# The moving weight operand of a hybrid decoder layer read in turns from two halves of a block

## The chip, the cores and the metric

The kernel runs on one NeuronCore of a Trainium2 chip. The metric is the device time of one execution in microseconds. Three executions of the kernel before took 367.40, 367.41 and 368.95 us; the median is 367.41 us.

## What is computed

One decoder layer on 256 rows of width 1024: an input projection, two attention mixers side by side, a gated merge, a feed-forward part, and a last norm. Cut to what matters here:

```python
h = rmsnorm(x, norm1_g)                       # x: 256 x 1024
proj = h @ w_in                               # 1024 x 4888: q, k/v, gates, q/k/v, merge gates
y_nsa, y_moba = nsa_attention(...), moba_attention(...)
mixed = sig(g_nsa) * (y_nsa @ w_up_nsa) + sig(g_moba) * (y_moba @ w_up_moba)
x = x + mixed @ w_out
u = relu(rmsnorm(x, norm2_g) @ w_ff1)         # 1024 x 4096
x = x + (u * u) @ w_ff2                       # 4096 x 1024
out = rmsnorm(x, norm_f_g)
```

All inputs are float32. Some 66 MB of weights pass through the core once.

## The kernel before

**Three products for one.** Every float32 operand of a large matrix product is split into a high part and a low part of type fp32r: ScalarE (ACT) copies the loaded block `raw` into `whi` (the copy rounds), VectorE (DVE) writes `wlo = raw - whi`. `mm3` (line 245) then issues three matmuls into one accumulator: high times high, high times low, low times high. Each goes through `mm` (line 242).

**Stationary and moving.** TensorE loads a 128x128 block first (LDWEIGHTS, engine PEld in the profile) and then streams the columns of the other operand past it (MATMUL, engine PE). A row `acc<-whi,hTh 128*128 128x512` reads: into `acc`, moving operand `whi` with 512 columns, stationary operand `hTh`. There are two kinds of stage, and only the first concerns the change:

- *The weights move.* `xstat` (line 256) multiplies the normed input, stationary in `hTh`/`hTl`, by the weight chunks `kva`, `kvb`, `q`, `qm`, `km`, `vm` (two chunks each). A chunk holds four blocks of `n` neighbouring columns, `n` = 384, 408 or 512, for four slices of the contraction; both halves of the 256 rows use each block. `seven_mms` (line 998) and `ff2_mms` (line 1039) multiply the squared activations, stationary in `ah`/`al`, by the chunks of `w_ff2`. `seven_mms` serves chunks 0 to 13: it forms seven products in place of eight, from blocks of 512 columns, three read from the chunk itself (`sh`, `sl`) and four from sums of its blocks (`wt`, split again into `whi`, `wlo`). `ff2_mms` serves the last two chunks without that. `mm3_halves` (line 250) is `mm3` with the 512 columns as two matmuls of 256; it stands at the end of a stage, so that half of a bank is complete earlier.
- *The weights stand still.* `wstat` (line 272) is used for the merge gates, the two up projections, `w_out` and `w_ff1`. There the activations move, 256 columns at a time.

**What sets the order.** The order is written by hand. Each chunk has a slot: `run_slot` (line 228) issues the slot's matmuls, and between them, at positions given as shares of the slot, the evacuations, splits and loads that `at` put into it. The engines run on their own behind semaphores. Loads go through SP's queue into three `raw` buffers, five chunks ahead; `whi` and `wlo` have three buffers each. From about 205 us on the slots alternate: one `w_ff1` chunk (48 matmuls, activations moving), then one `w_ff2` chunk (21 products of 512 columns, weights moving).

**The host's part.** `_layout` (line 1190) arranges the weights in HBM; `_blocks` cuts a matrix into chunks in which every partition's data lies in one run. The elementwise work on a chunk (splits, sums of blocks) treats all columns alike.

## Time and profile before

| view | value |
|---|---|
| device time, median of three | 367.41 us |
| span of the profiled execution, first to last instruction | 366.6 us |
| instructions | 6535 |
| DMA, mean over the span | 181 GB/s, 66.34 MB |
| stage 4.67 to 14.54 us, chunks kva (384 columns move) | 9.87 us, DMA share 1.02 |
| stage 14.54 to 29.80 us, kvb (408 columns move) and other work | 15.26 us, PE busy all of it |
| stage 82.92 to 211.04 us, weights mostly stationary | 128.12 us, PE busy 127.87 us |
| stage 344.49 to 360.00 us, the last two w_ff2 chunks and the end of the product | 15.51 us |

The profiled execution's own time lies 0.8 us above its span when it is taken as the median. [...]

### The profile page before, as it was taken

The numbers are of one execution on the slowest core, as the hardware profiler recorded it, in microseconds if no ns is written. First come the engines' busy times: TensorE is split into PE (matmuls) and PEld (weight loads), VectorE is DVE, ScalarE is ACT, GpSimd is POOL, SyncE is SP. The second block draws the span as 40 slices with busy tenths as digits, with TensorE's granted clock in tenths as the row PEclk, the third lists the DMA queues.
The fourth block names the chain that finished last, engine by engine and source line by source line (L and its number), as shares of the span: only waits on it lengthen the run. The fifth ranks groups of instructions, "written<-read, shape, count | busy, mean of one in ns | idle before, by whom it ended". The sixth has DMA issues, their size and how long they took to land.

```text
span 366.6 us, 6535 instructions
## 1 busy us (share of the span) xinstructions
PE 358.8 (98%) x2663; PEld 330.3 (90%) x2663; DVE 320.1 (87%) x466; ACT 241.4 (66%) x367; POOL 3.4 (1%) x14
## 2 busy tenths in 40 slices
PE   8999999999999999999999999999999999999993
PEld 7997877879999999999999999999999999999983
DVE  4988979998967759767978999999999999999985
ACT  5994765777746657625365988876766677766623
POOL 1010000000000000000000000000000000000000
PEclk9999999999999999999999999999999999999997
DMA  8978426333434333533483556544455665544003
GB/s 283 400 307 312 129 106 228 115 116 115 161 133 168 116 116 126 219 116 114 181 335 137 214 229 221 183 180 179 186 208 224 229 232 229 203 181 181 11 3 114
DMA packets 11262, 66.34 MB, mean 181 GB/s; under 512 B 1248, under 2 KB 2784, under 8 KB 3936
## 3 DMA queue, kind: packets, MB, share of 16 engines
q1 hardware_dynamic: 10368, 64.35, 47.3%
q10 hardware_dynamic: 864, 1.57, 1.2%
q8 instruction: 21, 0.34, 0.4%
q14 instruction: 9, 0.07, 0.1%
HBM read 64.87 MB, written 1.05 MB: 180 GB/s over the span
## 4 chain that ended last, share of the span: by engine, by line
PE 94%; issue 2%; ACT 1%; DVE 1%; POOL 0%; POOLq 0%; DVEq 0%
PE acc L243 61%; PE o L243 10%; PE yb L243 6%; PE tp L243 4%; PE qacc L243 3%; PE kvbacc L243 3%; PE Sa L243 2%; PE Sa L597 1%; PE tp L339 1%; ACT P L567 1%; PE yb L156 1%; PE Sb L597 1%; PE Sb L243 1%; PE o L886 0%; DVE P L581 0%
## 5 line engine op out<-in xcount | busy, mean ns | idle before, releaser
L116 DVE TENSOR_TENSOR wlo<-raw,whi 128x1024 fp32r<-128x1024 f32 (+3 forms) x83 | 104.9, 1285 | 3.3 <-ACT whi L114 3.2
L114 ACT ACTIVATE whi<-raw 128x1024 fp32r<-128x1024 f32 (+3 forms) x82 | 90.0, 1119 | 26.0 <-PE acc L243 11.9
L243 PE MATMUL acc<-h2h,whi 128*128 128x256 f32 x256 | 70.9, 277 | 0.0
L243 PE MATMUL acc<-h2l,whi 128*128 128x256 f32 x256 | 70.7, 276 | 0.0
L243 PE MATMUL acc<-h2h,wlo 128*128 128x256 f32 x256 | 70.7, 276 | 0.0
L243 PEld LDWEIGHTS acc<-h2h,whi 128*128 128x128 f32 x256 | 48.1, 188 | 0.0
L243 PEld LDWEIGHTS acc<-h2l,whi 128*128 128x128 f32 x256 | 48.1, 188 | 0.0
L243 PEld LDWEIGHTS acc<-h2h,wlo 128*128 128x128 f32 x256 | 48.1, 188 | 0.0
L989 ACT ACTIVATE whi<-wt 128x2048 fp32r<-128x2048 f32 x14 | 26.9, 1921 | 28.4 <-PE acc L243 27.3
L243 PE MATMUL acc<-hTh,wlo 128*128 128x256 f32 x128 | 36.6, 286 | 0.0
L243 PE MATMUL acc<-hTh,whi 128*128 128x256 f32 x128 | 35.5, 278 | 0.0
L243 PE MATMUL acc<-hTl,whi 128*128 128x256 f32 x128 | 35.5, 277 | 0.0
L991 DVE TENSOR_TENSOR wlo<-wt,whi 128x2048 fp32r<-128x2048 f32 x14 | 32.0, 2283 | 0.1
L243 PE MATMUL acc<-whi,hTh 128*128 128x512 f32 (+2 forms) x65 | 25.6, 394 | 0.1
L243 PE MATMUL acc<-wlo,hTh 128*128 128x512 f32 (+2 forms) x65 | 25.1, 386 | 0.0
L243 PE MATMUL acc<-whi,hTl 128*128 128x512 f32 (+2 forms) x65 | 24.8, 382 | 0.0
L982 DVE TENSOR_TENSOR sl<-raw,sh 128x1536 fp32r<-128x1536 f32 x14 | 24.5, 1749 | 0.0
L243 PEld LDWEIGHTS acc<-hTh,wlo 128*128 128x128 f32 x128 | 24.1, 188 | 0.2 <-issue 0.2
L243 PEld LDWEIGHTS acc<-hTh,whi 128*128 128x128 f32 x128 | 24.2, 189 | 0.1
L243 PEld LDWEIGHTS acc<-hTl,whi 128*128 128x128 f32 x128 | 24.0, 188 | 0.0
L980 ACT ACTIVATE sh<-raw 128x1536 fp32r<-128x1536 f32 x14 | 20.8, 1489 | 3.2 <-PE acc L243 3.2
L243 PE MATMUL acc<-mxh,whi 128*128 128x256 f32 x64 | 17.7, 276 | 0.0
(310 smaller groups left out, 868.6 us busy)
## 6 DMA issues: line engine op xcount, KB each, us to landing
raw<-in_ff_dram SPq DMA_DIRECT2D x32, 1024.0 KB, 5.1
raw<-in_gm_dram SPq DMA_DIRECT2D x8, 1024.0 KB, 4.8
raw<-in_wout_dram SPq DMA_DIRECT2D x4, 1024.0 KB, 4.8
raw<-in_q_dram SPq DMA_DIRECT2D x2, 1024.0 KB, 5.4
raw<-in_qm_dram SPq DMA_DIRECT2D x2, 1024.0 KB, 6.4
raw<-in_km_dram SPq DMA_DIRECT2D x2, 1024.0 KB, 6.0
raw<-in_vm_dram SPq DMA_DIRECT2D x2, 1024.0 KB, 4.8
raw<-in_upn_dram SPq DMA_DIRECT2D x2, 1024.0 KB, 4.8
```

The lines of the kernel that those rows point to most:

```text
L114: act.activation(hi[c][:, a:b], raw[c][:, a:b], AF.Copy)
L116: dve.tensor_tensor(lo[c][:, a:b], raw[c][:, a:b], hi[c][:, a:b].bitcast(F32), op=ALU.subtract)
L156: pe.transpose(warm[:, 0:128], ident, ident)
L243: pe.matmul(o, l, r, start=start, stop=stop, skip_group_check=True)
L339: pe.transpose(tp[:, j * 256 + t * 128:j * 256 + t * 128 + 128], src[:, t, (2 * i + j) * 128:(2 * i + j + 1) * 128], ident)
L567: act.activation(P[:, 2 * x + j, a:b], S[:, j, x], AF.Exp, scale=0.125, bias=st[:, 1, i:i + 1], accum_out=st[:, 2, i:i + 1])
L597: pe.transpose(T[:, j, x, o:o + 128], P[:, 2 * x + j, c:c + 128], ident)
L980: act.activation(singles[c][0], v, AF.Copy)
L982: dve.tensor_tensor(singles[c][1], v, singles[c][0].bitcast(F32), op=ALU.subtract)
L989: act.activation(hi[c], v, AF.Copy)
L991: dve.tensor_tensor(lo[c], v, hi[c].bitcast(F32), op=ALU.subtract)
```

## The change

In HBM, every block of `n` columns of the chunks `kva`, `kvb`, `q`, `qm`, `km`, `vm` and `ff2` is rearranged: its even columns first, its odd columns behind them. In SBUF a block thus holds column 0, 2, 4, ... in its first half and 1, 3, 5, ... in its second. The matmuls in which these weights move read the two halves in turns, so that the columns come in their old order: first half, second half, first half and so on, two neighbouring reads lying `n/2` elements apart (1024 bytes at `n` = 512, 768 at 384, 816 at 408). The outputs in PSUM stand as before. The number of instructions, their order on every engine, the sizes of all transfers and all tiles are the same. The matmuls of 256 columns read 128 columns from each half of the block.

```diff
+    def paired(v):
+        return v.rearrange("p (a b) -> p b a", a=2)
+
     def mm(o, l, r, start, stop):
+        if len(r.shape) > len(o.shape):
+            o = o.rearrange("p (b a) -> p b a", a=2)
         pe.matmul(o, l, r, start=start, stop=stop, skip_group_check=True)
...
     def mm3_halves(o, lh, ll, rh, rl, first, last):
         r = mm3(o, lh, ll, rh, rl, first, last)[:int(first)]
-        return r + [m for x in (slice(0, 256), slice(256, 512))
-                    for m in mm3(o[:, x], lh, ll, rh[:, x], rl[:, x], first, last)[int(first):]]
+        return r + [m for x in range(2)
+                    for m in mm3(o[:, 256 * x:256 * x + 256], lh, ll,
+                                 *(v[:, 128 * x:128 * x + 128] for v in (rh, rl)),
+                                 first, last)[int(first):]]
...
-                r += f(accs[t][:, :n], lh, ll, h[:, k * n:(k + 1) * n],
-                       l[:, k * n:(k + 1) * n], kt == 0, kt == 7)
+                r += f(accs[t][:, :n], lh, ll, paired(h[:, k * n:(k + 1) * n]),
+                       paired(l[:, k * n:(k + 1) * n]), kt == 0, kt == 7)
...
             if kb < 3:
-                h, l = (x[:, kb * 512:(kb + 1) * 512] for x in singles[c])
+                h, l = (paired(x[:, kb * 512:(kb + 1) * 512]) for x in singles[c])
             else:
-                h, l = (x[c][:, (kb - 3) * 512:(kb - 2) * 512] for x in (hi, lo))
+                h, l = (paired(x[c][:, (kb - 3) * 512:(kb - 2) * 512]) for x in (hi, lo))
...
-            a = ((1, 0), (2, 3))[k][c0 // 512] * 512 + c0 % 512
-            r += mm3(ops[p][:, 0:n], ah[:, 2 * k + t], al[:, 2 * k + t], hi[c][:, a:a + n],
-                     lo[c][:, a:a + n],
+            a = ((1, 0), (2, 3))[k][c0 // 512] * 512
+            b = slice(c0 % 512 // 2, (c0 % 512 + n) // 2)
+            h, l = (paired(x[c][:, a:a + 512])[:, b] for x in (hi, lo))
+            r += mm3(ops[p][:, 0:n], ah[:, 2 * k + t], al[:, 2 * k + t], h, l,
...
+def _halves(a, n):
+    s = a.shape
+    return a.reshape(-1, n // 2, 2).swapaxes(1, 2).reshape(s)
...
+    for k, n in (("kva", 384), ("kvb", 408), ("q", 512), ("qm", 512), ("km", 512), ("vm", 512),
+                 ("ff2", 512)):
+        d[k] = _halves(d[k], n)
```

## The prediction

> **What bounds the kernel now.** I read the page first, its busy times and its slices.

> ```profile
> span 366.6 us, 6535 instructions
> PE 358.8 (98%) x2663; PEld 330.3 (90%) x2663; DVE 320.1 (87%) x466; ACT 241.4 (66%) x367; POOL 3.4 (1%) x14
> PE   8999999999999999999999999999999999999993
> ```

> TensorE has work in all but the first and the last slice, but a busy matmul may still wait inside its duration, so next comes the view of waits, for PE alone.

> ```profile
> PE yb L156 <- POOL ones L157: 1.4, 1, 1.4
> PE Sa L597 <- DVE P L581: 0.2, 1, 0.2
> ```

> These two are all that it names: PE waits 1.6 us for other engines, 1.4 of them before the program's first product. So every nanosecond added to a matmul's distance to the next one adds to the end, and only what PE leaves waiting elsewhere is hidden. The distances stand in the timeline of PE. In a slot of w_ff2:

> ```profile
> 335.60 0.39 PE L243 MATMUL o<-whi,ah 128*128 128x512 f32 x1
> 335.82 0.39 PE L243 MATMUL o<-wlo,ah 128*128 128x512 f32 x1
> ...
> 337.87 0.39 PE L243 MATMUL acc<-sl,ah 128*128 128x512 f32 x1
> 338.09 0.39 PE L243 MATMUL acc<-sh,al 128*128 128x512 f32 x1
> 338.32 0.28 PE L243 MATMUL tp<-whi,ah 128*128 128x256 f32 x1
> ...
> 339.03 0.29 PE L243 MATMUL acc<-h2h,whi 128*128 128x256 f32 x1
> ```

> From 335.60 to 338.32 lie twelve matmuls of 512 columns: 2.72 / 12 = 0.2267 us each. From 338.32 to 339.03 lie six of 256 columns whose moving operand is weights: 0.118 us each. In the stage of kva, at the program's start:

> ```profile
> 6.05 0.53 PE L243 MATMUL acc<-whi,hTh 128*128 128x384 f32 x1
> 6.37 0.53 PE L243 MATMUL acc<-wlo,hTh 128*128 128x384 f32 x1
> ...
> 7.33 0.41 PE L243 MATMUL acc<-wlo,hTh 128*128 128x384 f32 x1
> ...
> 9.16 0.33 PE L243 MATMUL acc<-whi,hTl 128*128 128x384 f32 x1
> ...
> 14.37 0.33 PE L243 MATMUL acc<-whi,hTl 128*128 128x384 f32 x1
> ```

> From 9.16 to 14.37 lie thirty matmuls of 384 columns: 0.1737 us each. (The first seven, up to 7.33, stand 0.32 us apart or more.) 512 against 384 columns gives 0.0530 us for 128 columns, so **0.414 ns for a column** and some 0.015 us for the matmul itself. The durations in the groups say the same of a column:

> ```profile
> L243 PE MATMUL o<-whi,ah 128*128 128x512 f32 x42 | 16.3, 389 | 0.0
> L243 PE MATMUL tp<-whi,al 128*128 128x256 f32 x26 | 7.3, 283 | 0.0
> ```

> (389 - 283) / 256 = 0.414 ns. This number is what the change can touch: how fast PE takes columns of a moving operand when neighbours no longer lie side by side.

> **The change part by part.** Nothing is removed, added or moved in the order of instructions. The bytes from HBM, the splits on ACT and DVE and the sums of blocks are elementwise on the same tiles, so their cost stays. The room that they have, by stage:

> ```profile
> 29.80:82.92 53.12, 53.12 (x304) 42.35 (x297) 47.42 (x102) 35.34 (x75) 0.00 (x0) 1.00 0.45 159
> 215.83:221.29 5.46, 5.46 (x50) 5.46 (x49) 5.46 (x10) 2.92 (x2) 0.00 (x0) 1.00 0.53 224
> 334.22:339.03 4.81, 4.81 (x26) 4.09 (x25) 4.81 (x3) 3.88 (x4) 0.00 (x0) 1.00 0.52 196
> ```

> The columns after the length are PE, PEld, DVE, ACT, POOL, clock, DMA share and GB/s. In the first and the third stage, where weights move, PE is busy throughout at full clock, DVE for 89 to 100% of the time, DMA near half. (The second is a slot of w_ff1 with weights stationary.) If PE gets slower here, the others have more time and nothing new is late. If PE got faster, DVE would be near the bound in the w_ff2 slots.

> What changes is the address pattern of 683 matmuls: 48 for kva (2 chunks x 8 x 3), 48 for kvb, 195 for q to vm (8 x 24, three of them cut in two), 332 in the fourteen slots of seven products, 60 in the last two chunks. Their columns: 48 x 384 + 48 x 408 + 192 x 512 + 14 x 21 x 512 + 48 x 512 = **311,424 columns**. At 0.414 ns these are 129 us of PE's time, over a third of the span.

> No row before shows PE reading a moving operand with such a step, so the price has to be bounded. [...] On the other side, one instruction of the trace reads SBUF with a step between neighbours: the reduction at line 434, which takes every 32nd element, four to a sum. Beside it a plain operation of as many elements, and a plain reduction:

> ```profile
> L325 DVE TENSOR_TENSOR ropa<-qtm,kc 128x128 f32<-128x128 f32 x6 | 1.7, 289 | 0.1
> L493 DVE TENSOR_REDUCE st<-pcs 128x16 f32<-128x240 f32 x1 | 0.4, 403 | 0.0
> L434 DVE TENSOR_REDUCE gsum<-ident 128x32 f32<-128x128 f32 x1 | 0.4, 369 | 0.0
> ```

> From 289 and 403 ns an element costs 114 / 112 = 1.02 ns and the fixed part is 159 ns. The strided one spends 369 - 159 = 210 ns on 128 elements, 1.64 ns each: 0.62 ns more, or 1.6 times as much. It is another engine and a small instruction, but it shows that a step is not free for every reader of SBUF. Carried to PE as a ratio it adds 0.6 x 129 = 77 us; as an addition, 0.62 x 311,424 = 193 us; as an absolute price of 1.64 ns for each element, (1.64 - 0.414) x 311,424 = 382 us. [...]

> Between ends this far apart I take the value of PE's own nearest row, its other read of SBUF:

> ```profile
> L243 PEld LDWEIGHTS acc<-h2h,whi 128*128 128x128 f32 x256 | 48.1, 188 | 0.0
> ```
> ```profile
> 333.54 0.28 PE L243 MATMUL acc<-h2h,whi 128*128 128x256 f32 x1
> ...
> 333.88 0.28 PE L243 MATMUL acc<-h2h,whi 128*128 128x256 f32 x1
> ```

> With stationary weights PE loads 128 columns for every matmul, three matmuls take 0.34 us, and PEld is never idle (5.46 of 5.46 us above): 0.113 us for a load, 0.88 ns for a column. A moving column takes half of that now. [...] **So I take twice the time for a column: +0.414 ns x 311,424 = +129 us.** It lies between the two milder carryings of the DVE row (77 and 193).

> What is hidden of it: the first seven matmuls of kva already stand 0.32 us apart or more, 0.83 ns for a column, so there the slower reading may show nothing: 7 x 384 x 0.414 ns = 1.1 us less. Waits of PE on splits and evacuations inside its busy time in the attention stages shrink when PE is slower, by about 1 us; the group there that stands worst has a mean of 404 ns against 389 in the w_ff2 slots, 47 x 15 ns = 0.7 us:

> ```profile
> L243 PE MATMUL acc<-whi,hTh 128*128 128x512 f32 x47 | 19.0, 404 | 0.0
> ```

> The sum: 366.6 + 129 - 2.1 = 493.5 us of span, 494 us with the 0.8 us that the median lies above the span.

> [...]

> **The rivals.**

> [...]

> *It gets faster.* The fixed part of a matmul differs by the kind of stage: with activations moving, 256 columns take 0.113 us, with weights moving 0.118. Such a difference could come from the two reads of PE, moving and loading, meeting in the same part of memory: the moving one runs through addresses at twice the pace and overtakes the other. Read in turns from two halves, it walks at the pace of the load and need never meet it. The whole excess is 9 us (358.4), the difference seen between the kinds 683 x 0.005 to 0.0067 = 3.4 to 4.6 us (363): I take 361 us. It decides if the step itself is free; then the point is whether the excess comes from the meeting of the two reads or from issuing. DVE, full in the w_ff2 slots, would give some of it back.

> [...]

> *A smaller loss.* Every second read only pays something, or the reader hides part: the DVE row's ratio gives 366.6 + 77 + 0.8 - 2 = 442 us; the case reaches from 370 to 480.

> *A larger loss.* Each element costs a full access of 1.64 ns, as in the DVE row taken absolutely: 366.6 + 382 - 2 = 747 us; with the additive carrying, 558. From 510 us upwards.

> *The change does not do what it says.* The pattern could be folded back into one run; it cannot, since the two halves are not neighbours in any order. This has no chance of its own.

> **How the numbers follow.** Twice the column time, 494 us, has 0.40; its own range is 484 (the fixed part goes as well) to 505 (a column at the load's 0.88 ns, +16 us less what is hidden). Free: 0.16. Faster: 0.20. A smaller loss: 0.12. A larger one: 0.12. Faster by over 0.5% (below 365.6; 0.5% is about what a measurement of this kernel tells from no change): 0.20. Within 0.5%: 0.16. Slower: 0.64. The range runs from 358 to 505 us; it leaves out the larger loss and some edges, 0.16 to 0.18 together. It is wide because cases of both signs have weight and the price of the step is not in the trace.

> **What would show it.** In the timeline of a w_ff2 slot the starts of matmuls of 512 columns should stand 0.43 to 0.45 us apart in place of 0.227, durations near 600 in place of 389 ns, and a slot of seven products take 9.2 us in place of 4.8; matmuls with moving activations keep 0.113 us. DVE's share should fall below 70%, with more idle time until PE. If the distances are 0.227, the step is free; at 0.215 to 0.22, the two reads had met; at 0.3 to 0.4, or over 0.8, the DVE row's ratio or its absolute price was the better guide. The prediction is wrong at its root if kva and q differ in the price of a column, since then the distance between the halves decides and not the step as such.

## The result and the profile after

| | before | after |
|---|---|---|
| device time, median of five each | 367.56 us (367.40 to 368.95) | 365.62 us (364.46 to 366.04) |
| span of the profiled execution | 366.6 us | 363.8 us |
| ratio after / before | | 0.9935, 95% interval 0.9913 to 0.9956 |

The change makes the kernel faster: by 0.65% in the ratio, by 1.9 us between the medians. The forecast was 494 us. The page of the kernel after, its span, busy times, PE's slices and the chain that ended last (shares by engine):

```profile
span 363.8 us, 6533 instructions
PE 352.8 (97%) x2663; PEld 328.7 (90%) x2663; DVE 319.6 (88%) x466; ACT 240.3 (66%) x367; POOL 3.4 (1%) x14
PE   7989999999999999999999999999999999999992
...
PE 69%; DVE 18%; ACT 4%; issue 3%; DMA 3%; SPq 0%; POOLq 0%; POOL 0%; DVEq 0%; ACTq 0%
```

PE is busy 6.0 us less, and the work of DVE is what it was. PE now has gaps in the first tenth, and the chain, which had 94% of PE before, has 18% of DVE and 3% of DMA. The timeline of PE in a w_ff2 slot (start, duration, what):

```profile
331.56 0.38 PE L249 MATMUL o<-whi,ah 128*128 128x512 f32 x1
331.78 0.38 PE L249 MATMUL o<-wlo,ah 128*128 128x512 f32 x1
...
334.58 0.38 PE L249 MATMUL acc<-sh,al 128*128 128x512 f32 x1
334.80 0.27 PE L249 MATMUL tp<-whi,ah 128*128 128x256 f32 x1
```

A matmul of 512 columns lasts 0.38 us here, and the next one starts some 0.22 us after it started; so what one costs PE is counted from start to start. From 331.56 to 334.80 lie fifteen matmuls: 3.24 / 15 = **0.216 us each, in place of 0.2267**. The groups by shape (busy us, mean ns of one) say the same as durations:

```profile
L249 PE MATMUL o<-whi,ah 128*128 128x512 f32 x42 | 15.9, 379 | 0.0
L249 PE MATMUL tp<-whi,al 128*128 128x256 f32 x26 | 7.1, 275 | 0.0
```

389 became 379 and 283 became 275 ns. All the rearranged matmuls lose alike: 384 columns go from 0.1735 to 0.162 us between starts, 408 from 0.186 to 0.1725. For 683 matmuls at some 11 ns that is 7.4 us of PE's time. The last matmul, however, ends at 357.25 in place of 360.46 us, 3.2 us earlier (the spans differ by 2.8 us, the medians by 1.9). Where the rest stayed shows in PE's waits (us in total, times, longest):

```profile
PE tp L418 <- ACT kcd L320: 1.0, 2, 0.5
PE tp L249 <- DVE al L949: 0.7, 1, 0.7
PE acc L249 <- ACT qtm L323: 0.5, 1, 0.5
...
PE acc L249 <- DVE wlo L116: 0.2, 1, 0.2
```

Before, there were two waits. And by stretches (length, then PE, PEld, DVE, ACT, POOL busy, clock, DMA share, GB/s):

```profile
14.35:25.55 11.20, 10.16 (x62) 9.49 (x61) 9.40 (x19) 9.18 (x17) 0.97 (x1) 1.00 0.87 335
25.55:80.99 55.44, 54.95 (x372) 45.84 (x372) 51.04 (x115) 37.34 (x75) 0.00 (x0) 1.00 0.50 180
325.27:330.92 5.65, 5.65 (x51) 5.52 (x50) 5.65 (x8) 3.50 (x3) 0.00 (x0) 1.00 0.85 344
330.92:335.47 4.55, 4.55 (x27) 4.07 (x26) 4.55 (x5) 3.66 (x4) 0.00 (x0) 1.00 0.20 29
```

- kvb grew from 10.27 to 11.20 us: in this execution PE is ahead of the loads. The chain passes here through `DMA raw<-in_q_dram`, 6.92 us from 12.86 on, and q starts at 25.55 us, before at 24.81. In the traces of two later kernels with the same distances (groups of 8 and of 128) it starts at 24.29 and 24.10, so this stage differs from one execution to another.
- q to vm shrank from 57.40 to 55.44 us, 1.96 of the 2.1 us that 195 matmuls can give.
- A w_ff2 slot takes 4.55 in place of 4.81 us, but seven of the thirteen w_ff1 slots behind one take 5.64 to 5.76 in place of 5.46. The thirteen pairs of slots take 131.64 in place of 133.45 us, 10.13 in place of 10.27 each.
- The end, from 344.49 before and from 341.15 after, kept its 16 us: its first product waits 0.7 us for DVE's `al`.

The long w_ff1 slots have two causes. Up to 300 us PE waits for nothing there: in every second slot all 48 matmuls stand 117.7 to 117.9 ns apart, in the others some 113.5, as in every slot before the change. The groups of the slots from 224.05 and from 234.26 us, in this order:

```profile
L249 PE MATMUL acc<-h2h,whi 128*128 128x256 f32 x16 | 4.5, 281 | 0.0
L249 PE MATMUL acc<-h2h,whi 128*128 128x256 f32 x16 | 4.4, 276 | 0.0
```

This is 0.2 us a slot, about 1.0 us over the thirteen. What stretches them is open. From 305 us on PE waits for DVE at the start of a w_ff1 slot, some 0.6 us in all. Such a wait, in the timeline of all engines:

```profile
333.49 2.28 DVE L116 TENSOR_TENSOR wlo<-raw,whi 128x2048 fp32r<-128x2048 f32 x1
...
335.59 0.28 PE L249 MATMUL acc<-h2l,whi 128*128 128x256 f32 x1
335.69 2.28 DVE L999 TENSOR_TENSOR wlo<-wt,whi 128x2048 fp32r<-128x2048 f32 x1
335.82 0.19 PEld L249 LDWEIGHTS acc<-h2h,wlo 128*128 128x128 f32 x1 [0.16 <-DVE wlo L116]
```

The load of the low part of w_ff1 waits until DVE has written it, and DVE goes straight on to the next split. DVE's own pace shows in two starts of the same operation, one pair of slots apart, first before and then after the change:

```profile
323.13 1.75 DVE L982 TENSOR_TENSOR sl<-raw,sh 128x1536 fp32r<-128x1536 f32 x1
333.35 1.75 DVE L982 TENSOR_TENSOR sl<-raw,sh 128x1536 fp32r<-128x1536 f32 x1
```
```profile
321.59 1.75 DVE L990 TENSOR_TENSOR sl<-raw,sh 128x1536 fp32r<-128x1536 f32 x1
331.81 1.75 DVE L990 TENSOR_TENSOR sl<-raw,sh 128x1536 fp32r<-128x1536 f32 x1
```

It is 10.22 us in both. Before, PE needed 10.27 us for a pair, so DVE drew slowly ahead of it; now PE catches up with DVE and from then on takes DVE's pace.

### The profile page after: what moved, and what is told of

Its sections match the earlier page's. It is cut to its first block, busy times and chain, and to the rows that moved or that the text cites. A ratio compares the mean times of both kernels' runs of the same rounds, so it can differ in the third digit from the quotient of the medians.

```text
span 363.8 us, 6533 instructions
## 1 busy us (share of the span) xinstructions
PE 352.8 (97%) x2663; PEld 328.7 (90%) x2663; DVE 319.6 (88%) x466; ACT 240.3 (66%) x367; POOL 3.4 (1%) x14
## 4 chain that ended last, share of the span: by engine, by line
PE 69%; DVE 18%; ACT 4%; issue 3%; DMA 3%; SPq 0%; POOLq 0%; POOL 0%; DVEq 0%; ACTq 0%
PE acc L249 47%; PE o L249 7%; DVE wlo L116 6%; PE yb L249 4%; PE qacc L249 3%; PE tp L249 2%; DMA raw<-in_q_dram 2%; ACT P L575 2%; DMA gx<-in_gx_dram 1%; DVE sl L990 1%; PE Sa L605 1%; DVE wlo L999 1%; PE Sa L249 1%; DVE al L949 1%; DVE ust L565 1%
## 5 line engine op out<-in xcount | busy, mean ns | idle before, releaser
L249 PEld LDWEIGHTS acc<-h2h,wlo 128*128 128x128 f32 x256 | 48.1, 188 | 0.3 <-DVE wlo L116 0.2
L249 PEld LDWEIGHTS acc<-h2h,whi 128*128 128x128 f32 x256 | 48.1, 188 | 0.0
L249 PE MATMUL acc<-whi,hTh 128*128 128x512 f32 (+2 forms) x65 | 24.6, 378 | 0.9 <-ACT qtm L323 0.5
L249 PE MATMUL acc<-wlo,hTh 128*128 128x512 f32 (+2 forms) x65 | 24.1, 370 | 0.2 <-DVE wlo L116 0.2
L249 PE MATMUL acc<-whi,hTl 128*128 128x512 f32 (+2 forms) x65 | 23.8, 366 | 0.0
```

The costliest lines, as they stand in the source:

```text
L249: pe.matmul(o, l, r, start=start, stop=stop, skip_group_check=True)
```

## Experiments on where the gain went

All compare with runs of the kernel before on the same chip (medians 367.8 to 368.0 us). A letter names a theory that the expectation spells out.

**One stage at a time.** The rearrangement and the read in turns for some chunks alone; the edit for kva and kvb (the two others read `('q', 'qm', 'km', 'vm')` and `('ff2',)`, the latter with the reads of w_ff2 as in the change):

```diff
+PAIRED = ('kva', 'kvb')
...
+                pr = paired if CHUNKS[c][0] in PAIRED else (lambda v: v)
...
-    for k, n in (("kva", 384), ("kvb", 408), ("q", 512), ("qm", 512), ("km", 512), ("vm", 512),
-                 ("ff2", 512)):
+    for k, n in (("kva", 384), ("kvb", 408),):
```

> Only the chunks kva and kvb are rearranged and read in turns; q to vm and w_ff2 as before. Theory (PE's saving counts only where PE is the last to be ready; this stage waits for its loads): 96 matmuls save 12 to 14 ns each, 1.2 us, but the end moves by 0 to -0.5 us, since q's first block lands no earlier. Rival (every saved nanosecond of PE counts): -1.2 us.

Measured: 367.89 us, ratio 1.0001 [0.9978, 1.0024]. The distances fell, the median did not, and the rival of a full gain in the median fell. The single times spread from 366.4 to 371.8 us, those of the kernel before from 367.5 to 368.9. The trace is of an execution of 366.52 us, and in it q starts at 23.42 us, 1.4 earlier than before: here the gain arrives, while other executions take longer than any of the kernel before. That the loads make the difference fits the chain of the result, but is not shown for each execution.

> Only q, qm, km and vm are rearranged and read in turns. Theory: PE is the bound here, 195 matmuls at 0.216 in place of 0.227 us, -2.1 us, of which about -1.8 reach the end. Rival (DVE, 89% busy there, takes it back): -1 us or less.

Measured: 366.36 us, ratio 0.9956 [0.9943, 0.9969]; the stage takes 55.44 us, as after the whole change. Here PE's gain is the kernel's.

> Only w_ff2 is rearranged and read in turns. 392 matmuls save 11 ns each, 4.2 us of PE. Theory (DVE becomes the bound of a pair of slots at about 10.13 us against 10.27): the end moves by -1.2 to -1.6 us, and PE waits for DVE's low parts at the start of every second w_ff1 slot. Rival (PE stays the bound): -4 us.

Measured: 366.58 us, ratio 0.9965 [0.9951, 0.9978]. Of the 392 matmuls x 11 ns = 4.3 us that PE saves here, some 1.7 arrive in the trace. The rival of a full gain fell. The expectation put the loss down to waits for DVE in every second w_ff1 slot. The trace has such waits in the last four slots only, from 306 us on; up to there every second slot is stretched as after the change (117.7 to 117.9 ns). In the runs of kva/kvb alone and of q to vm alone no slot is: the stretch comes with the reading of w_ff2 in turns, though the operands of w_ff1 are as before.

**DVE relieved.** In each slot of seven products the four sums of activation blocks (DVE, 0.28 us each) are replaced by one copy on ACT, so the products use other numbers there; once on top of the change, once on the kernel before.

```diff
-        a_sum(4, 0, 2, ALU.add)
-        a_sum(5, 1, 0, ALU.subtract)
+        act.activation(aq[:, 4:8], aq[:, 0:4], AF.Copy)
...
-        a_sum(6, 4, 1, ALU.subtract)
...
-        a_sum(7, 3, 6, ALU.subtract)
```

> The changed kernel without the four sums of squared activations in each of the 14 slots of seven products: one ACT copy of 512 columns stands in their place, so those products are formed from other numbers. DVE has 1.1 us less to do in each pair of slots. Theory (DVE is the bound of a pair of slots at 10.13 us): a pair falls to PE's own 5.45 + 4.55 = 10.0 us, the starts of the w_ff1 slots no longer wait, 1.5 to 2.5 us less than the change. Rival (PE's own distances stretch for another reason): no difference to the change.

> The same in the kernel before the change. Theory: PE is the bound there, a pair stays at 10.27 us and the time at 367.5 to 368 us. Rival (DVE bound already): 1 us or more less.

Measured: with the change 362.49 us, ratio 0.9852 [0.9833, 0.987]; on the kernel before 367.98 us, ratio 1.0000 [0.9987, 1.0013]. The stretch from 210 to 310 us of the first, then of the kernel after, then of the kernel before:

```profile
210.00:310.00 100.00, 100.00 (x716) 95.27 (x715) 97.06 (x73) 78.32 (x75) 0.00 (x0) 1.00 0.56 210
```
```profile
210.00:310.00 100.00, 100.00 (x713) 95.15 (x712) 99.97 (x109) 73.98 (x64) 0.00 (x0) 1.00 0.56 210
```
```profile
210.00:310.00 100.00, 100.00 (x698) 92.80 (x697) 99.97 (x107) 74.88 (x65) 0.00 (x0) 1.00 0.55 206
```

DVE's share falls from 99.97 to 97.06 of 100 us. But the kernel before shows 99.97 as well, and there the relief gains nothing: the share does not tell which engine is the bound. The spans of the first two differ by 3.0 us. Of these, 1.5 lie before the first w_ff2 slot; q starts at 23.68 us in the one trace and at 25.55 in the other. The thirteen pairs take 131.28 in place of 131.64 us, not the 130 of the expectation: every second w_ff1 slot still takes 5.65 us, and PE waits for nothing in it, so here the rival was right. Behind the pairs lie 1.2 us; PE no longer waits for `al`. So the relief is worth some 1.5 us after the change and nothing before it: **DVE holds back a part of what PE gained, from 305 us on.** In the pairs PE's own stretch stands close behind DVE. The change, w_ff2 alone and groups of 8 all take 131.64 to 131.66 us, however many of their slots are stretched (groups of 8 has two); with DVE relieved the stretch alone still holds them at 131.28.

## Experiments on what a column pays for

These change only the order in which a block of `n` columns lies in HBM and how its columns are then read; the products are the same. The edits are one line in `paired` and its counterparts in `mm` and `_halves`. "Distance" is the usual one between starts of 512-column matmuls in the w_ff2 slots.

**Four places in turns.**

```diff
-        return v.rearrange("p (a b) -> p b a", a=2)
+        return v.rearrange("p (a b) -> p b a", a=4)
```

> As the change, but every block is cut in four (columns 0, 4, 8, ... first, then 1, 5, 9, ...), and the moving read takes the four quarters in turns. Theory M (the saving comes from the moving read walking no faster than the load of the next weights, so that they do not meet): the moving read now walks at half the load's pace, the load overtakes it, and a matmul of 512 columns is back at 0.227 us or more. Rival R (a run of neighbours is itself what stalls, any reading in turns cures it): 0.216 us and the time of the change, about 365.6 us. [...]

Measured: 397.76 us, ratio 1.0808 [1.0794, 1.0822], distances of 272 to 284 ns. Theory M's "or more" covers this; R fell. What two places give is not what four give. The group, with its duration of 442 ns against 379:

```profile
L249 PE MATMUL o<-whi,ah 128*128 128x512 f32 x42 | 18.6, 442 | 0.0
```

**The two places close together.** Groups of 8 columns (two neighbouring fours of columns, 16 bytes each, in turns) and groups of 128 (places 256 bytes apart; of 8 for kvb):

```diff
-        return v.rearrange("p (a b) -> p b a", a=2)
+        g = 8
+        return v.rearrange("p (g a b) -> p g b a", a=2, b=g // 2)
```

> As the change, but the even and odd columns are parted within every group of eight: four even ones, then four odd ones, and the read takes the two fours in turns, 16 bytes apart. The read runs through a block at the old pace. Theory M (what helps is that the moving read walks at the pace of the load): the excess stays, 0.227 us per matmul of 512 columns, 367.5 us. Rival R2 (what helps is that neighbouring reads lie apart, the distance is of no matter): 0.216 us and 365.6 us. A third outcome, over 0.23 us, would say that two near places are worse than two far ones.

> The same with groups of 128 columns: 64 even ones, then 64 odd ones, in turns, 256 bytes apart (kvb in groups of eight). Within a group of 512 bytes the read walks at the load's pace, from group to group it jumps. Theory M: 0.216 to 0.222 us, partly cured. Rival R2: 0.216 us. If lines8 gives 0.227 and this 0.216, the distance decides and lies between 16 and 256 bytes.

Measured: 364.12 us, ratio 0.9896 [0.9874, 0.9917], and 364.87 us, 0.9916 [0.9889, 0.9943]; 216 ns in both.

```profile
L250 PE MATMUL o<-whi,ah 128*128 128x512 f32 x42 | 15.9, 379 | 0.0
```

M fell. The distance between the two places does not count, be it 16, 256 or 1024 bytes (216 ns in each), and neither does how fast the read walks through the block: groups of 8 are walked in order, as fast as before the change.

**Where the stationary block lies.** The gap ahead of `ah`/`al` grows from 64 to 128 elements, so that the load starts at the same place within 512 bytes as the moving weights.

```diff
-                FB["p"].tile([128, 64], F32, name="gap3")
+                FB["p"].tile([128, 128], F32, name="gap3")
```

> The changed kernel with the unused tile gap3 of 128 in place of 64 elements: the stationary ah and al of the w_ff2 slots lie 256 bytes further, so that they start at the same place within 512 bytes as the moving weights. [...] Rival R2: they stay at 0.216 us, and so does the time, 365.6 us.

Measured: 365.45 us, ratio 0.9932 [0.9909, 0.9954], 216 ns. No sign of a meeting of the two reads at this place.

**Steps inside four columns.** Groups of four, in the order 0, 2, 1, 3:

```diff
-        return v.rearrange("p (a b) -> p b a", a=2)
+        return v.rearrange("p (g a b) -> p g b a", a=2, b=2)
```

> Even and odd columns are parted within every group of four: 0, 2, 1, 3 in memory, read 0, 1, 2, 3, so that neighbouring reads lie 8 bytes apart or, at every second step, 4, always within 16 bytes until the group ends. Theory R2 (neighbouring reads have to lie on different pieces of 16 bytes): the excess is back, 0.227 us, 367.8 us. Rival R3 (the form of the access decides: a pattern of several dimensions is issued differently from a plain run, wherever it points): 0.216 us, 365 us.

Measured: 368.15 us, ratio 1.0003 [0.999, 1.0016], 227 ns, the duration as before the change:

```profile
L250 PE MATMUL o<-whi,ah 128*128 128x512 f32 x42 | 16.3, 389 | 0.0
```

A pattern with a step is by itself worth nothing here: 227 ns (R3 fell). R2 in the form that the elements in turn come from different fours of columns (the 16 bytes of groups of 8) held up to here; the next runs test it further.

**Runs from each half.** Four neighbours from one half, then four from the other; and two and two:

```diff
-        return v.rearrange("p (a b) -> p b a", a=2)
+        return v.rearrange("p (a b e) -> p b a e", a=2, e=4)
```

> The two halves of a block are read in turns by fours: four neighbouring columns of 16 bytes from the first half, four from the second. Three of four reads follow their neighbour as in a plain run, yet the pattern is not a run. Theory R2: 0.227 us, or half cured, 0.222. Rival R3: 0.216 us.

> As runs4, with two neighbouring columns (8 bytes) from the first half, then two from the second. Theory R2 (what counts is that neighbouring reads change the piece of 16 bytes): half of them do, so between 0.216 and 0.227 us, about 0.222. Rival (what counts is how many pieces a stretch of eight reads visits one after the other, as runs4 suggests with 0.246 to 0.254): 0.216 if two pieces in turns are fine in any order within eight reads, over 0.23 if not.

Measured: fours 379.82 us, ratio 1.0326 [1.0301, 1.035], 246 to 254 ns; twos 429.50 us, ratio 1.1666 [1.1634, 1.1698], 333 ns. No expectation had these numbers. The twos, in durations:

```profile
L249 PE MATMUL o<-whi,ah 128*128 128x512 f32 x42 | 21.1, 501 | 0.0
```

The twos are far worse than the ones of the change (333 against 216 ns), though neighbours lie together. That ruled out "neighbours must differ" and "neighbours must agree" alike, and suggested a count: take every second column of a matmul in the order of reading (0, 2, 4, ... or 1, 3, 5, ...), and count how many of them in a row come from the same four neighbours in memory. Read in turns from two halves these are all four; in plain order two; with twos in turns one. The four is the author's estimate from two runs, groups of 8 (216 ns) and of four (227 ns); why it, or every second column, should matter was not shown. The count was formed after these runs, so two more were made to test it.

**Leaving a four early.** As the change, but each half is walked with a step of two elements in two passes, or of four in four:

```diff
-        return v.rearrange("p (a b) -> p b a", a=2)
+        return v.rearrange("p (a b q) -> p q b a", a=2, q=2)
```

> As the change, but each half is walked with a step of two elements: in two passes, the even elements of both halves in turns, then the odd ones. Neighbouring reads lie in different pieces of 16 bytes as in the change, but each piece is left after two elements in place of four. [...] Rival R2 (that neighbours lie in different pieces is all that counts): 216 ns, 365.6 us.

> As the change, but each half is walked with a step of four elements, in four passes: every element lies in another piece of 16 bytes than any of its neighbours in time. [...] Rival R2: 216 ns, 365.6 us.

Measured: step two 368.00 us, ratio 1.0002 [0.9991, 1.0012], 227 ns; step four **504.37 us**, ratio 1.3699 [1.3678, 1.3719], 451 ns. First the group of step two, then the timeline of step four:

```profile
L249 PE MATMUL o<-whi,ah 128*128 128x512 f32 x42 | 16.3, 389 | 0.0
```
```profile
480.10 0.63 PE L249 MATMUL acc<-whi,ah 128*128 128x512 f32 x1
480.55 0.64 PE L249 MATMUL acc<-wlo,ah 128*128 128x512 f32 x1
481.00 0.63 PE L249 MATMUL acc<-whi,al 128*128 128x512 f32 x1
```

R2 (different neighbours suffice: 216 in both) fell. By the count step two takes two in a row, as plain order does, and it has plain order's 227 ns. Step four takes one, and is slower, as the others with one are; but its 451 ns lie far outside the 272 to 333 of quarters and twos. The runs together:

| elements in a row from the same four, of every second column | kernels | distance, ns |
|---|---|---|
| four | the change, groups of 8 and of 128 | 216 |
| two | before, order 0 2 1 3, step two | 227 |
| two, then to the other half | fours in turns | 246 to 254 |
| one, but the four is met again soon | quarters, twos in turns | 272 to 284, 333 |
| one, and the four is left for long | step four | 451 |

The count puts four, two and one in order, but it does not give the sizes. By it fours in turns take two in a row, as plain order does, and yet need 19 to 27 ns more; single elements cost from 272 to 451. The conditions in the last three rows ("then to the other half", "met again soon", "left for long") were put in to fit these runs and were not tested by themselves. No view shows a cause behind the count. What is shown is the distance of each order, and that alternating between two places costs nothing by itself (216 ns).

## Experiments on the load beside the matmul

**A load that steps.** In the kernel before, the stationary blocks of w_ff2 are read with a step of seven elements (four in the last two chunks), so that the products take mixed blocks of activations.

```diff
-            r += f(P[name], ah[:, ka], al[:, ka], h, l, i == 0, last)
+            sh, sl = (a.rearrange("p k q -> p (k q)")[:, ka:896:7] for a in (ah, al))
+            r += f(P[name], sh, sl, h, l, i == 0, last)
```

> The kernel before the change, moving reads plain. In the w_ff2 slots the stationary operand is read with a step of 7 elements through the tile of seven blocks (4 in the last two chunks), so that every element of the load lies on another piece of 16 bytes; the products are formed from mixed blocks. Theory D (the excess is a disturbance between the two reads): the 0.227 us of these matmuls changes, to 0.216 if the load now stays out of the way, or upwards. Rival A (the moving read stalls by itself): 0.227 us, unless the load gets so slow that it binds, which its own duration of 188 ns would show by rising over 250.

Measured: 382.71 us, ratio 1.0395 [1.0366, 1.0424]; distances of 233 to 250 ns at 512 columns and 233 to 235 (from 120) at 256. The group of its weight loads:

```profile
L243 PEld LDWEIGHTS o<-whi,ah 128*128 128x128 f32 x44 | 13.9, 317 | 0.0
```

317 ns in place of 188. Matmuls of 256 and of 512 columns now stand about equally far apart, so the load is their bound: 233 / 128 = 1.82 ns an element, about twice the 0.88 of before. As the load became the bound, this run cannot tell D from A.

**A short load.** In the kernel before, the third product of each slot product loads 32 columns in place of 128.

```diff
+            o = P[name]
...
+                  lambda o=o[0:32], s=al[:, ka][:, 0:32], h=h: mm(o, s, h, False, last)]
```

> The kernel before, and in the w_ff2 slots of seven products the product with the low part of the activations loads 32 stationary columns in place of 128, so it leaves out that part for the other 96 rows (and the last product is not cut in two). The load runs beside the matmul ahead of it, that of the low part of the weights. Theory D (the 11 ns by which a plain matmul of 512 columns exceeds 216 come from the load of the next stationary beside it, in step with it): a quarter of the load leaves about a quarter of the excess, so of the three distances of each product the one after the low weights falls from 227 to about 219 ns, the two others stay at 227; 98 of them, 0.8 us. Theory A (the excess is the moving read's own, whatever is loaded beside it): all three stay at 227 ns, and the time within 0.1% of before.

Measured: 368.70 us, ratio 1.0020 [1.0009, 1.0030]. The distances behind the three matmuls of a product became 229, 233 and 232 ns, in the order in which they run (high weights, low weights, high weights with the short load), where 227, 219, 227 (D) or 227 three times (A) was expected. The loads in the timeline:

```profile
337.17 0.19 PEld L243 LDWEIGHTS o<-wlo,ah 128*128 128x128 f32 x1
337.40 0.11 PEld L243 LDWEIGHTS o<-whi,al 128*32 128x32 f32 x1
337.62 0.19 PEld L243 LDWEIGHTS o<-whi,ah 128*128 128x128 f32 x1
```

The load did become shorter, and no matmul gained; the one beside the short load, for which D gave 219, is the longest. So the load's length is not what the 11 ns measure. That all three distances rise by 1 to 6 ns suggests that the load beside a matmul does have a say, but the short product also writes 32 rows in place of 128, and the run does not part the two. Both theories missed, and how the load enters stays open.

## Experiments towards a faster version

**Activations in turns too.** The stages in which the activations move get the same: rows `q` and `q + 128` lie apart and are read in turns, and the evacuations of `w_out` and `w_ff1` put the rows into place as they read PSUM.

```diff
-            r += mm3(o, hi[c][:, a:a + 128], lo[c][:, a:a + 128], ah[:, k, :], al[:, k, :],
+            r += mm3(o, hi[c][:, a:a + 128], lo[c][:, a:a + 128], paired(ah[:, k, :]), paired(al[:, k, :]),
...
-                act.activation(r[:, m], outs[m], AF.Relu)
+                act.activation(r[:, m].rearrange("p (a b) -> p a b", a=2),
+                               outs[m].rearrange("p (b a) -> p a b", a=2), AF.Relu)
```

> The changed kernel, and the activations that move past stationary weights are read in turns too: row q and row q + 128 of 256, from the layout as it is. Merge gates and up projections keep the row order that this gives, the residual add and the squares put the rows back while they read PSUM. [...] Rival (these matmuls are bound by the load of 128 columns, whatever the moving read does): 0.113 us, 365.6 us, or 1 to 2 us more if the evacuations get slower by the strided read.

Measured: **362.34 us** (362.23 to 363.96), ratio 0.9868 [0.9845, 0.9892]. The mean distance of 256 columns with activations moving is 111.7 ns, from 113.4, so the rival's 0.113 us did not stand. The merge gates take 62.36 us (from 63.06), the up projections 24.57 (24.93), `w_out` 21.44 (21.76). From 250 us on a pair of slots takes 10.22 us, DVE's own pace, no less than after the change:

```profile
210.00:310.00 100.00, 99.74 (x715) 93.83 (x714) 99.97 (x112) 72.29 (x63) 0.00 (x0) 1.00 0.55 206
```

In these slots the load of the weights waits for DVE's `wlo` twelve times, 3.1 us in all. This version beats both kernels. Of the 3.4 us between its span and that of the change, 1.4 lie in the three stages above and 2.0 before q starts (23.58 against 25.55 us), where the activations' order has no part.

**The sums on GpSimd.** On top of that, the four activation sums of a slot go from DVE to POOL.

```diff
-            dve.tensor_tensor(aq[:, o], aq[:, x], aq[:, y], op=op)
+            pool.tensor_tensor(aq[:, o], aq[:, x], aq[:, y], op=op)
```

> h_paired, and the four sums of squared activations in each slot of seven products on POOL in place of DVE; every result as the reference's. Theory (DVE is the bound of a pair of slots, 10.13 us, with 1.1 us of it in these sums): a pair falls towards PE's 5.36 + 4.55 = 9.91 us, 2 to 3 us less than h_paired, about 360 us. Rival (POOL and DVE hinder each other in SBUF, or the sums come too late for ah): no gain or a loss of 1 to 5 us against h_paired.

Measured: 367.61 us, ratio 0.9988 [0.9973, 1.0003]: 5.3 us lost again between the medians, the rival's loss. The groups of POOL and DVE (mean ns of one), and PE's largest wait:

```profile
L977 POOL TENSOR_TENSOR aq<-aq 128x128 f32<-128x128 f32 x56 | 79.2, 1433 | 233.3 <-ACT aq L941 232.2
...
L1003 DVE TENSOR_TENSOR wlo<-wt,whi 128x2048 fp32r<-128x2048 f32 x14 | 35.2, 2518 | 0.1
...
L979 DVE TENSOR_TENSOR wt<-raw 128x1024 f32<-128x1024 f32 x14 | 20.2, 1440 | 0.0
```
```profile
PE acc L249 <- DVE wlo L116: 5.0, 12, 0.8
```

A sum takes POOL 1433 ns where DVE took 284, and in the same slots DVE's own operations stretch: the split of the sums from 2283 to 2518 ns, the first sum of blocks from 1216 to 1440, the low part of the activations (`al`) from 1083 to 1324. A pair of slots takes 10.59 us. Why they stretch no view shows.

## Why the prediction was wrong, step by step

*PE bounds the kernel.* Right: relief for DVE gained nothing there (ratio 1.0000).

*683 matmuls, 311,424 columns, 0.414 ns each.* Right, and the condition "wrong at its root if kva and q differ in the price of a column" did not occur: they lose alike. (The range's upper end does not follow from its own terms: 494 + 16 us is 510, less what is hidden of it, and not 505.)

*The failed step: "So I take twice the time for a column".* It carried the load's 0.88 ns over to a moving column whose neighbours lie apart; no run shows this price for the change. The runs show another thing in its place: with neighbours 1024 bytes apart a matmul of 512 columns takes 216 ns, less than the 227 of plain order and not 430, and with 16 or 256 bytes between them it is the same. Neighbours in time need not lie side by side. What costs, by the runs together, is the order in which neighbours in memory are taken: step four takes one of four neighbours and goes on, and stands at 451 ns, 0.88 ns a column, which is the load's figure, and at 504 us, near the forecast of 494. That is agreement in a number, for a kernel that is not this one; the load itself reads neighbours in plain order, so such a walk is not what makes its 0.88 ns. **The nearest row was read for its number, without the condition under which it arises.**

*The DVE row of line 434.* It reads four places in turns, 32 elements apart, and walks each in order. That is the order of the run with four places, not of the change: PE paid 272 to 284 ns for it in place of 227, 1.2 to 1.25 times, where the DVE row gave 1.6. For two places it is no bound.

*"The whole excess is 9 us".* This term, some 13 ns for each of the 683 matmuls, gives the lower end of the range, 358 us; no run shows it. What the runs show in its place is a fall by 10.7 ns, from 226.7 to 216, and 7.4 us for all rearranged matmuls.

*"It gets faster".* The way was right, and PE's gain of 7.4 us lies between the 3.4 to 4.6 and the 9 us that this rival gave. Its reason was not: that the read walks at the load's pace is contradicted by groups of 8, which are walked at the old pace, and of the two reads meeting the moved gap shows no sign, all at 216 ns. *"If the distances are 0.227, the step is free"*: they are 0.216, so it costs nothing and gains besides. The sentence that DVE "would give some of it back" was right: of PE's 7.4 us, 3.2 reached the end of the last product. The stages say where: kva and kvb gained in some executions and lost in others, q to vm gave about all, and of the 4.3 us of w_ff2 the thirteen pairs kept 1.8. There PE's own stretch in the w_ff1 slots took about 1.0 and waits for DVE 0.6; behind them came 0.7 for `al`.

*"What is hidden of it", 2.1 us.* It was the cover for a slower PE and has no object here. The same slack read the other way, how little the loads and DVE were ahead of PE, would have bounded the gain.

## What to carry to other kernels

Where TensorE's moving operand is of type fp32r, lies in neighbouring columns, and PE is the bound, two places read in turns were worth some 5% of a matmul of 512 columns (227 to 216 ns), provided that the order of columns can be changed for nothing (here in HBM) and that each place is walked in order; a walk through both halves with a step of four columns doubled the price (451 ns). Before a price is borrowed from another row, ask what in that row makes it, and whether the new access has the same. And a gain on the bound engine is worth no more than the lead of the next one. The busy share does not show how near the next one is (DVE had 99.97% from 210 to 310 us before and after); the time from an operation's start to its start in the next round does: 10.22 us for DVE against 10.27 for PE.
